# A transformer block on one core: all engines' instruction order taken from a simulated timeline

## The chip, the core and the metric

The kernel runs on one core of a Trainium2 chip. A core has five engines that each work through a queue of their own in order: TensorE (PE in the rows, with its weight loads as PEld), VectorE (DVE), ScalarE (ACT), GpSimd (POOL) and SyncE (SP), which here only starts DMA transfers. They wait for each other by semaphores. The metric is the device time of one execution in microseconds (us), as the median of several executions of the same program.

## What is computed

The reference is one block of a bidirectional encoder in float32, with 512 tokens, 16 learned meta tokens added (528 in all) and a model width of 1024. Cut to what matters:

```
h = concat([meta_tokens, x])
h = h + 0.5 * swiglu(rms_norm(h), w_gate, w_up, w_down)      # FFN 1, inner width 2816
z = rms_norm(h) @ w_in                                       # 10 parts, split by columns
y_a = hgrn2_bidir(...)      # gated linear recurrence, 4 heads of 128, both directions
y_b = axial_gqa(...)        # 8 query heads of 64 over 2 key heads, softmax over 528 keys
mixed = sigmoid(zgate_a) * (y_a @ w_up_a) + sigmoid(zgate_b) * (y_b @ w_up_b)
h = h + mixed @ w_out
h = h + 0.5 * swiglu(rms_norm(h), w_gate2, w_up2, w_down2)   # FFN 2
return h[meta:]
```

In `swiglu` the gate goes through silu and is multiplied with the up projection before the down projection. In `hgrn2_bidir` a head's gates come from sigmoids, and its recurrence is computed in chunks of 128 tokens.

## The kernel before

Everything is kept transposed: features on the 128 partitions, tokens along the free axis. A float32 product is made of three products of rounded parts: each weight tile `raw` (128 x 1024) is loaded by SP, rounded to `whi` by ACT (L84, the copy) and its remainder `wlo` is formed by DVE (L85, the subtraction). The activations are split in the same way (`xh`, `xl`). PE then multiplies `whi` with `xh`, `whi` with `xl` and `wlo` with `xh` into one PSUM bank (helper `group`, L197). `raw`, `whi` and `wlo` have two buffers each.

The program has three stages.

- **FFN 1** (function `ffn`): the first four columns of the inner width are plain groups. The other 18 are taken two at a time by `pair`, which forms the gate and up projections of two columns by a scheme with seven half-size products instead of eight (L374, products of 12 matmuls over 264 tokens each). The weights that it needs are partly sums of loaded tiles (`seven`, with sums on DVE at L110, L111, L117 and on POOL at L116). A down projection follows after each group of columns.
- **The mix**: the projections `w_in`, attention (`score`, `turned`, `product`) and the recurrence (`gla_head`, `gla_out`) are interleaved on PE by the class `Interleave`, with latencies given by hand (`LAT_...`). For this stage PE's order is the order in which the program is written; the other engines are left to the scheduler.
- **FFN 2**: as FFN 1, with 512 tokens.

What the names stand for that come up below: `R` is the reciprocal root of the mean square of a token (matmul with ones at L302, square root at L303, reciprocal at L304), by which each projection is multiplied when it leaves PSUM (L543). For a query, its squares (`tq`, L668) are summed by PE at L676, a Newton iteration on tiny tiles follows (`rsqrt`, L556 to L563: `xq`, `yq`, `aq`), and the rotary positions (`rope`, L600 to L603); `qst` holds the split query (L684, L685). A score is the bank pair `S` (L695); its maximum is `nm` (L699), its exponential `pr` (L704), its row sum `sm` (L706). The transposed `pr` goes from the bank `at` (L719) to `ph` and `pl` (L722, L723). In the recurrence a level copies `ks` (L882, ACT), multiplies it into the only bank `gs` (L886), multiplies `Z` on (L875 on DVE, L873 on POOL) and takes `gs` over into `A` by a predicated copy (L890). At the end of a head, `on` and `st` (L921, L927 to L929) feed the products of L940. The head's gates are the sigmoids of L810 and L811:

```
both = ap(Z, 0, ((3 * T, 2), (1, T)))
act.activation(both, both, AF.Sigmoid, scale=-1.0)
act.activation(Z[:, 1:3], zi, AF.Sigmoid)
```

Exponentials and sigmoids need different function tables on ACT; an ACT_TABLE_LOAD stands ahead of the first after a switch.

The order of the work is set in this way. The program is written once as one sequence. The tile framework gives every instruction its buffers and waits, and a scheduler then chooses each engine's order from the instructions whose operands it takes to be ready, those written first (or marked as of high priority, `OFFSET`) ahead. It goes by a simple estimate of when an operand is ready. In the mix PE is exempt: `tc.manual_schedule(engines={pe.engine})` (L528).

## Time and profile before

| what | value |
|---|---|
| median of 3 runs | 1199.37 us (1198.83 to 1202.58) |
| the profiled execution, whole | 1202.23 us |
| its span in the trace | 1200.4 us |
| PE busy | 1170.7 us, 98% of the span |
| DVE, ACT, POOL busy | 852.5, 583.3 and 188.2 us |
| loaded and stored | 106.22 MB, 88 GB/s on the mean |

The profiled execution is 1.83 us longer than its span (what lies before the first and behind the last instruction), and 0.24% above the median of the runs. PE is busy nearly all the time; whether another engine matters is to be read from the stretches in which PE is not.

### The profile page before, as it was taken

What the parts mean: (1) busy time and instruction counts of PE and PEld (TensorE: products, weight loads), DVE (VectorE), ACT (ScalarE), POOL (GpSimd) and SP (SyncE); (2) the same over time, 40 slices, a digit from 0 to 9 for tenths busy, and PEclk for the clock granted to TensorE, in tenths of its full rate; (3) what the DMA queues carried; (4) which work ended last, traced back from release to release, by engine and by line L of the source; (5) the groups of instructions that cost most, each with busy time, mean ns of one, the idle gap of its engine ahead of it and who ended that gap; (6) DMA issues with size and microseconds to landing.
All of it is one profiled execution on the core that took longest, in us unless ns stands there. A gap on an engine that the chain in (4) does not pass through costs nothing.

```text
span 1200.4 us, 19411 instructions
## 1 busy us (share of the span) xinstructions
PE 1170.7 (98%) x7765; PEld 1071.8 (89%) x7765; DVE 852.5 (71%) x1349; ACT 583.3 (49%) x984; POOL 188.2 (16%) x153
## 2 busy tenths in 40 slices
PE   8999999999999999999999999999999999999998
PEld 8999999999999788878888788888878998998997
DVE  7988748848956868787686735455788956866863
ACT  5545425524545475756557433334444633543541
POOL 1012001001102023243232410122001101101100
PEclk9999999999999999999999999999999999999999
DMA  6233222332223221111111113232413332333213
GB/s 233 63 100 136 89 89 96 108 95 90 80 67 120 70 71 36 53 36 54 36 54 36 61 46 112 81 118 94 156 55 121 104 102 97 107 100 108 90 54 123
DMA packets 34234, 106.22 MB, mean 88 GB/s; under 512 B 3936, under 2 KB 4320, under 8 KB 34144
## 3 DMA queue, kind: packets, MB, share of 16 engines
q1 hardware_dynamic: 33984, 104.44, 26.3%
q8 instruction: 61, 1.00, 0.3%
q0 software_dynamic: 160, 0.54, 0.1%
q14 instruction: 29, 0.24, 0.1%
HBM read 102.87 MB, written 2.10 MB: 87 GB/s over the span
## 4 chain that ended last, share of the span: by engine, by line
PE 81%; DVE 10%; ACT 5%; issue 2%; DMA 1%; POOL 0%; SPq 0%; ACTq 0%; DVEq 0%; POOLq 0%
PE mm L197 31%; PE mm L374 15%; PE at L374 9%; PE at L197 5%; PE gs L374 4%; PE am L197 4%; PE S L197 4%; PE am L374 2%; DVE wlo L85 2%; PE gs L886 2%; ACT whi L84 1%; PE mm L940 1%; PE mm L734 1%; PE S L695 1%; PE at L719 1%
## 5 line engine op out<-in xcount | busy, mean ns | idle before, releaser
L84 ACT CAST whi<-raw 128x1024 fp32r<-128x1024 f32 (+2 forms) x220 | 189.4, 862 | 286.4 <-PE mm L197 121.2
L85 DVE TENSOR_TENSOR wlo<-raw,whi 128x1024 fp32r<-128x1024 f32 (+2 forms) x220 | 225.1, 1025 | 27.8 <-ACT whi L84 22.3
L197 PE MATMUL mm<-xh,whi 128*128 128x512 f32 (+1 forms) x504 | 166.7, 364 | 5.5 <-ACT xh L278 2.2
L197 PE MATMUL mm<-xl,whi 128*128 128x512 f32 (+1 forms) x504 | 159.8, 351 | 0.5 <-DVE xl L279 0.5
L197 PE MATMUL mm<-xh,wlo 128*128 128x512 f32 (+1 forms) x504 | 159.1, 349 | 0.0
L116 POOL TENSOR_TENSOR sums<-raw 128x512 f32<-128x512 f32 x36 | 58.8, 1634 | 492.7 <-DVE wlo L85 492.7
L197 PEld LDWEIGHTS mm<-xh,whi 128*128 128x128 f32 x504 | 89.9, 191 | 18.5 <-ACT xh L278 2.4
L84 ACT CAST whi<-sums 128x1024 fp32r<-128x1024 f32 x72 | 75.4, 1051 | 62.3 <-DVE sums L111 20.9
L85 DVE TENSOR_TENSOR wlo<-sums,whi 128x1024 fp32r<-128x1024 f32 x72 | 87.6, 1219 | 24.9 <-ACT whi L84 24.7
L197 PEld LDWEIGHTS mm<-xh,wlo 128*128 128x128 f32 x504 | 89.0, 190 | 12.7 <-issue 0.2
L197 PEld LDWEIGHTS mm<-xl,whi 128*128 128x128 f32 x504 | 89.5, 191 | 10.6 <-DVE xl L279 1.0
L873 POOL TENSOR_TENSOR Z<-Z,tot 128x512 f32<-128x512 f32 x32 | 46.9, 1467 | 158.2 <-PE gs L886 94.4
L197 PE MATMUL mm<-hh,wlo 128*128 128x256 f32 (+1 forms) x218 | 63.0, 334 | 0.0
L197 PE MATMUL mm<-hh,whi 128*128 128x256 f32 (+1 forms) x218 | 62.8, 333 | 0.1
L197 PE MATMUL mm<-hl,whi 128*128 128x256 f32 (+1 forms) x218 | 62.9, 332 | 0.0
L374 PE MATMUL mm<-xl,whi 128*128 128x264 f32 (+1 forms) x216 | 61.3, 284 | 0.0
L374 PE MATMUL mm<-xh,whi 128*128 128x264 f32 (+1 forms) x216 | 61.2, 283 | 0.0
L374 PE MATMUL mm<-xh,wlo 128*128 128x264 f32 (+1 forms) x216 | 61.1, 283 | 0.0
L468 DVE SCALAR_TENSOR_TENSOR h<-mm,h 128x512 f32<-128x512 f32 (+2 forms) x40 | 21.0, 545 | 41.5 <-PE mm L197 41.5
L374 PE MATMUL at<-xh,whi 128*128 128x264 f32 (+1 forms) x144 | 42.0, 292 | 0.0
L197 PEld LDWEIGHTS mm<-hh,wlo 128*128 128x128 f32 x218 | 37.2, 188 | 4.5 <-DVE wlo L85 0.7
L197 PEld LDWEIGHTS mm<-hh,whi 128*128 128x128 f32 x218 | 37.4, 188 | 4.2 <-ACT whi L84 0.5
(365 smaller groups left out, 3377.7 us busy)
## 6 DMA issues: line engine op xcount, KB each, us to landing
raw<-in_wg SPq DMA_DIRECT2D x43, 512.0 KB, 3.7
raw<-in_wu SPq DMA_DIRECT2D x43, 512.0 KB, 3.2
raw<-in_w_in SPq DMA_DIRECT2D x42, 512.0 KB, 3.2
raw<-in_wd SPq DMA_DIRECT2D x48, 384.0 KB, 3.1
raw<-in_wd SPq DMA_DIRECT2D x16, 256.0 KB, 2.6
raw<-in_wup SPq DMA_DIRECT2D x16, 256.0 KB, 2.6
raw<-in_wout SPq DMA_DIRECT2D x8, 512.0 KB, 3.2
h<-in_xT SPq DMA_DIRECT2D x4, 528.0 KB, 6.6
```

The lines of the kernel that those rows point to most:

```text
L84: nc.scalar.copy(hi[:, c], src)
L85: nc.vector.tensor_tensor(lo[:, c], src, hi[:, c].bitcast(F32), ALU.subtract)
L116: nc.gpsimd.tensor_tensor(t[:, E], r0[:, E], r1[:, E], ALU.add)
L197: pe.matmul(o, a[:, sl], b[:, cols], start=(k == 0 and i == 0), stop=(k == n - 1 and i == 2))
L374: pe.matmul(o, a[:, sl], b[:, kk, :], start=(start and kk == 0 and i == 0), stop=(kk == 3 and i == 2), skip_group_check=True)
L468: dve.scalar_tensor_tensor(h[c][:, cols], o, 0.5, h[c][:, cols], ALU.mult, ALU.add)
L695: pe.matmul(s[:, WIDE][:, cols], st[e][:, c * P:(c + 1) * P], kk[:, cols], start=(i == 0), stop=(i == 1))
L719: pe.transpose(o[:, k, :], pr[:, k * P:(k + 1) * P], ident)
L734: pe.matmul(av, v[:, k, :], p[:, k, :], start=(k == 0 and i == 0), stop=False)
L873: pool.tensor_tensor(xx, xx, first, ALU.mult)
L886: pe.matmul(s[:, c, :], ks[:, c * P:(c + 1) * P], ap(Z, T + c * P, ((2 * m, P // (2 * m)), (T + m, 2), (1, m))), start=True, stop=True)
L940: pe.matmul(o[:, c, :], a, b, start=(i == 0), stop=(i == len(terms) - 1))
```

## The change

One argument is added where the tile context is made. The scheduler then runs a timeline of all engines as it goes, with an assumed duration for each instruction, and takes an operand to be ready when that timeline says so. It does so for all engines and all three stages. No instruction is added to or taken from the program, but for function tables on ACT: their number depends on the order.

```diff
-    with tile.TileContext(nc) as tc:
+    with tile.TileContext(nc, schedule_with_timeline_sim=True) as tc:
```

In the mix PE's order stays as it was written from the first query's sums (L676) to shortly before the stage's end. All other orders move: of the 1,300 to 1,350 rows of DVE most stand elsewhere by a few places.

**PE at the start of the first pair of FFN 1.** `mm_2162`, `mm_2163` and `mm_2164` are three banks of one pair, `whi_2075` and `wlo_2076` the parts of its first weight, `whi_2179` and `wlo_2180` those of its third, a sum; the rows begin where the last down projection ends. Before:

```order
L374 MATMUL mm_2162<-b11h_293,whi_2075 128x264
L374 MATMUL mm_2162<-b11l_294,whi_2075 128x264
L374 MATMUL mm_2162<-b11h_293,wlo_2076 128x264
L374 MATMUL mm_2162<-b11h_293,whi_2075 128x264
L374 MATMUL mm_2162<-b11l_294,whi_2075 128x264
```

And with the change:

```order
L374 MATMUL mm_2162<-b11h_293,whi_2075 128x264
L374 MATMUL mm_2162<-b11l_294,whi_2075 128x264
L374 MATMUL mm_2163<-b21h_295,whi_2075 128x264
L374 MATMUL mm_2163<-b21l_296,whi_2075 128x264
L374 MATMUL mm_2164<-n1h_297,whi_2179 128x264
L374 MATMUL mm_2164<-n1l_298,whi_2179 128x264
L374 MATMUL mm_2164<-n1h_297,wlo_2180 128x264
L374 MATMUL mm_2164<-n1h_297,whi_2179 128x264
L374 MATMUL mm_2164<-n1l_298,whi_2179 128x264
L374 MATMUL mm_2162<-b11h_293,wlo_2076 128x264
```

Seven matmuls that need no `wlo_2076` now stand ahead of the first that needs it, where `mm_2162` and `mm_2163` had been finished one after the other.

**ACT in the first head of the recurrence**, from the second score's scaled maximum on. Before:

```order
L701 ACTIVATE nr<-nm,yq 128x1
L810 ACT_TABLE_LOAD
L810 ACTIVATE Z<-Z 128x2x528
L704 ACT_TABLE_LOAD
L704 ACTIVATE pr,sm<-S,nr,yq 128x528
L722 CAST ph<-at 128x4x128
L707 ACTIVATE pr<-pr,sm 128x528
L811 ACT_TABLE_LOAD
L811 ACTIVATE Z<-zi 128x1056
L701 ACTIVATE nr<-nm,yq 128x1
L84 CAST whi<-raw 128x1024
L704 ACT_TABLE_LOAD
```

And with the change:

```order
L811 ACT_TABLE_LOAD
L811 ACTIVATE Z<-zi 128x1056
L810 ACTIVATE Z<-Z 128x2x528
L701 ACTIVATE nr<-nm,yq 128x1
L704 ACT_TABLE_LOAD
L704 ACTIVATE pr,sm<-S,nr,yq 128x528
L707 ACTIVATE pr<-pr,sm 128x528
L722 CAST ph<-at 128x4x128
L84 CAST whi<-raw 128x1024
L701 ACTIVATE nr<-nm,yq 128x1
```

The two sigmoids stand together, both ahead of the second exponential, and two of four table loads are gone (19 in the whole program before, 17 now).

**DVE in the second head of the recurrence**, between the products of the recurrence's levels (`gs_5891`, `gs_5931`), the rotary positions of a query (`tm_5659`, `tq_5878`) and two scores (`S_5900`, `S_5951`). Before:

```order
L602 SCALAR_TENSOR_TENSOR tq_5878<-tq_5878,par_92,cossin_4480 128x512
L561 TENSOR_TENSOR aq_5865<-yq_5864 128x8
L875 TENSOR_TENSOR Z_5088<-Z_5088,tot_5089 128x132x4
L562 SCALAR_TENSOR_TENSOR aq_5865<-aq_5865,xq_5863 128x8
L603 TENSOR_TENSOR tm_5659<-tm_5659,tq_5878 128x512
L563 SCALAR_TENSOR_TENSOR yq_5864<-aq_5865,yq_5864 128x8
L723 TENSOR_TENSOR pl_5832<-at_5940,ph_5831 128x4x128
L561 TENSOR_TENSOR aq_5865<-yq_5864 128x8
L699 TENSOR_REDUCE nm_5956<-S_5951 128x1
L562 SCALAR_TENSOR_TENSOR aq_5865<-aq_5865,xq_5863 128x8
L890 COPY_PREDICATED A_5732<-msk_64,gs_5931 128x512
```

And with the change:

```order
L890 COPY_PREDICATED A_5732<-msk_64,gs_5891 128x512
L601 SCALAR_TENSOR_TENSOR tm_5659<-tm_5659,par_92,cossin_4480 128x512
L602 SCALAR_TENSOR_TENSOR tq_5878<-tq_5878,par_92,cossin_4480 128x512
L699 TENSOR_REDUCE nm_5905<-S_5900 128x1
L559 TENSOR_SCALAR yq_5864<-yq_5864 128x8
L603 TENSOR_TENSOR tm_5659<-tm_5659,tq_5878 128x512
L561 TENSOR_TENSOR aq_5865<-yq_5864 128x8
L875 TENSOR_TENSOR Z_5088<-Z_5088,tot_5089 128x132x4
L890 COPY_PREDICATED A_5732<-msk_64,gs_5931 128x512
```

The predicated copy that empties the bank of `gs_5931` now follows directly on its `Z` product; the Newton steps and the next score's maximum that had stood between come behind it. The maximum of the score before, `nm_5905`, has gone the other way, behind L601 and L602.

## Rows read from the trace of the kernel before

**Rows 1.** The page: span, and busy time of each engine.

```profile
span 1200.4 us, 19411 instructions
...
PE 1170.7 (98%) x7765; PEld 1071.8 (89%) x7765; DVE 852.5 (71%) x1349; ACT 583.3 (49%) x984; POOL 188.2 (16%) x153
```

**Rows 2.** Busy time by stretch: us, PE, PEld, DVE, ACT, POOL, granted clock, DMA share, GB/s.

```profile
0.00:25.00 25.00, 21.12 (x135) 20.06 (x135) 17.57 (x25) 15.76 (x25) 4.63 (x7) 0.93 0.72 259
25.00:85.00 60.00, 59.67 (x481) 59.00 (x481) 54.78 (x115) 28.88 (x53) 0.93 (x1) 1.00 0.28 88
85.00:380.00 295.00, 293.64 (x2383) 291.65 (x2382) 212.91 (x306) 137.27 (x212) 36.06 (x24) 1.00 0.29 94
380.00:672.00 292.00, 271.44 (x1706) 237.57 (x1705) 216.23 (x405) 179.92 (x339) 79.25 (x77) 0.98 0.16 53
672.00:1160.00 488.00, 487.80 (x2876) 431.84 (x2875) 335.02 (x480) 213.05 (x345) 67.37 (x44) 1.00 0.29 96
```

**Rows 3.** PE's waits over the span: engine waited for, us in total, times, longest.

```profile
PE gs L886 <- ACT ks L882: 3.1, 3, 2.5
PE S L695 <- ACT pr L704: 2.7, 3, 1.6
PE S L695 <- DVE qst L685: 2.5, 1, 2.5
PE gs L886 <- ACT qst L684: 2.3, 1, 2.3
...
PE mm L940 <- DVE st L929: 2.1, 1, 2.1
...
PE at L374 <- DVE wlo L85: 1.4, 2, 0.7
```

**Rows 4.** Timeline at 184 us: start, us, engine, line, operation; idle before and releaser.

```profile
182.72 1.30 POOL L116 TENSOR_TENSOR sums<-raw 128x512 f32<-128x512 f32 x1 [4.16 <-DVE wlo L85]
182.84 2.26 DVE L85 TENSOR_TENSOR wlo<-raw,whi 128x1024 fp32r<-128x1024 f32 x1
...
185.16 0.39 PE L374 MATMUL at<-b11h,wlo 128*128 128x264 f32 x1 [0.65 <-DVE wlo L85]
...
186.31 1.21 DVE L85 TENSOR_TENSOR wlo<-sums,whi 128x1024 fp32r<-128x1024 f32 x1
```

**Rows 5.** Timeline at 436 us.

```profile
436.00 1.28 ACT L704 ACT_TABLE_LOAD   x1
...
437.30 0.79 ACT L704 ACTIVATE pr<-S,nr,yq 128x528 f32<-128x528 f32 x1
...
438.23 0.51 PE L695 MATMUL S<-kh,qst 128*128 128x256 f32 x2 [1.58 <-ACT pr L704]
```

**Rows 6.** Timeline at 465 us.

```profile
464.37 0.70 DVE L875 TENSOR_TENSOR Z<-Z,tot 128x528 f32<-128x528 f32 x1
...
465.60 0.60 ACT L882 COPY ks<-Z 128x512 f32<-128x512 f32 x1
...
466.26 1.01 PE L886 MATMUL gs<-Z,ks 128*128 128x128 f32 x3 [2.51 <-ACT ks L882]
```

**Rows 7.** Timeline at 532 us.

```profile
531.32 0.72 DVE L890 COPY_PREDICATED A<-msk,gs 128x512 f32<-128x512 uint8 x1
...
532.18 0.57 PE L886 MATMUL gs<-Z,ks 128*128 128x128 f32 x3 [2.29 <-ACT qst L684]
```

**Rows 8.** Timeline from 382 to 406 us.

```profile
382.13 3.45 DVE L304 RECIPROCAL R<-R 128x528 f32<-128x528 f32 x1
...
387.43 0.63 ACT L668 ACTIVATE tq<-tm 128x512 f32<-128x512 f32 x1 [2.77 <-DVE tm L543]
...
389.12 0.95 PE L676 MATMUL mm<-kones,tq 128*128 128x2 f32 x8
...
397.86 0.77 PE L197 MATMUL mm<-xh,whi 128*128 128x256 f32 x2 [1.22 <-ACT tm L623]
...
405.28 0.47 PE L197 MATMUL mm<-xh,whi 128*128 128x512 f32 x1 [1.05 <-DVE Z L543]
```

## The prediction

> **What bounds the kernel now.** I read the page first. PE is busy for 1170.7 of 1200.4 us [rows 1], so a new order can at best take away the 29.7 us in which it isn't. The table of stretches tells where they are: from 380 to 672 us, the mix with attention and recurrence, PE is busy for 271.44 of 292 us, so 20.6 us of the 29.7 lie there; from 85 to 380 us 1.4 us, from 672 to 1160 us 0.2 us, and 3.9 us in the first 25 us [rows 2]. DVE (216 of 292) and ACT (180 of 292) are far from full in the mix, so the idle time there is one of order and latency: an operation that PE needs stands behind others in DVE's or ACT's queue. That is what the change touches. In the FFNs it can only keep what is there or lose.
>
> The table of PE's waits gives the sizes: three waits of gs for ks, 3.1 us in all, of which one is 2.5; three of a score for the exponential before it, 2.7 us; one of a score for qst, 2.5; one at a gs put down to qst, 2.3; one for st, 2.1; and in FFN 1 two for wlo, 1.4 us [rows 3]. For each I looked at the timeline and then at what stands there in the changed order.
>
> **The change part by part.** No instruction is added, so every term is a wait that shrinks, grows or moves. The sum goes against the profiled execution of 1202.23 us.
>
> *Starts of pairs, FFN 1.* At 185.16 us PE waits 0.65 us for a wlo subtraction that took 2.26 us [rows 4]. An undisturbed one took 1.21; a POOL sum ran from 182.72 to 184.02, beside the first half of it [rows 4]. The Trainium skill ("SBUF — State Buffer", Who interferes with whom) has a DVE instruction with two inputs from SBUF blocked by a GpSimd one that reads SBUF, until that ends. The 2.26 us agree with it: 1.18 left of POOL's operation and 1.21 of its own would make 2.4. A scheduler whose assumed durations lack this places a wlo about 1 us early, and that rule is the strongest thing that speaks against the change (rival 3). In the changed order seven matmuls without that wlo stand ahead at the first pair, against two before. At the rate of the second stretch (481 in 59.67 us, 0.124 us each [rows 2]) five more cover 0.62 us. At the 0.65 us wait the changed order likewise puts five matmuls and a product's start ahead. Both waits go: -1.3 us (from 0 to -1.4).
>
> *Start and first columns.* DVE is busy for 54.8 of 60 us from 25 to 85 us, with 0.33 us of idle time on PE [rows 2]. The new order has DVE form all eight normalised tiles early, which pushes three wlo subtractions 2 to 4 us back, close to where PE needs them; matmuls of hi parts are pulled ahead as cover. I take +0.5 us. The bounds are 0 and three waits as long as the longest for wlo, 0.7 [rows 3], so +2.
>
> *Start of the mix.* The matmuls of the mean square (L302) go 18 places back on PE: eight of double width and ten at 0.124 us, about 3.2 us. Before, the reciprocal ran from 382.13 to 385.58, ACT squared the query from 387.43 to 388.06, and PE took it at 389.12 [rows 8]. A reciprocal that ends at 388.8, with its evacuation (about 0.65) and 0.63 for the square, gives 390.1: a new wait of 1.0 us. But the next wait of this chain, 1.22 us at 397.86 for a square root [rows 8], shrinks by as much, since that chain has not become later. Two evacuations that PE needs at 405.28 (1.05 us [rows 8]) and shortly after have moved ahead of wlo subtractions by about 4 us, and their waits go. I take -1.2 us (from +1.0, if only the delay shows, to -1.7).
>
> *Tables in the first head.* The wait of 1.58 us at 438.23 is for an exponential, ahead of which ACT loads a table for 1.28 us [rows 5]. With the sigmoids together that load is gone: -1.3 us. The exponential before it now has both sigmoids ahead, and by the durations of the rows ends about 0.5 us later: +0.5. Together -0.8 us (from +0.5 to -1.8). The Trainium skill ("ScalarE: Activation LUTs", What ACT_TABLE_LOAD costs) puts a switch at 1.28 us of load and 1.38 us of drain; the trace has the load, but the exponential starts 0.02 us behind it [rows 5], so no such drain shows as time after it. By the page the term would be -2.2 us.
>
> *First long wait for ks.* PE stands for 2.51 us until 466.26. The Z product ended at 465.07, but ACT took the copy only at 465.60, behind an exponential, and DVE had done a score's maximum first [rows 6]. In the changed order the copy stands ahead of the exponential and the product ahead of the maximum, about 0.7 to 1 us earlier. A copy from 464.4 to 465.0 instead of 465.60 to 466.20: -1.3 us (from 0 to -2.5, bounds of the row).
>
> *The bank of gs.* At 532.18 PE waits 2.29 us. The table names qst, but that is no operand of this matmul; the predicated copy that frees the only gs bank ended at 532.04 [rows 7]. It now stands before the tiny Newton steps and the next maximum, and by the rows' durations ends 2.3 us or more earlier: -2.0 us (at most -2.3). The maximum nm_5905 pays for it; its exponential then ends at about 526.7, 0.5 us before the next score needs the bank. If that is missed by its neighbour's stretch of about 1 us, the term keeps -1.5.
>
> *The wait for st* (2.1 [rows 3]): the addition comes about 0.8 us sooner, the copy ahead of it later, which moves part of the wait to the matmul before: -0.8 us (from 0 to -2.1). *The wait for qst* (2.5 [rows 3]): the rotary sum is earlier, but a subtraction and an evacuation still stand ahead on DVE: -0.7 us (from 0 to -2.5).
>
> The mix thus gives -1.2 - 0.8 - 1.3 - 2.0 - 0.8 - 0.7 = -6.8 us. Where PE comes sooner it meets the next wait sooner, and the three waits of scores for exponentials show that this chain has little slack [rows 3]; I take it that a third is given back, +2.3. With the FFN terms: -1.3 + 0.5 - 6.8 + 2.3 = -5.3 us. 1202.23 - 5.3 = 1196.9; the profiled execution is 0.24% above the median, so the median becomes 1194. All lower bounds together make some -14 us (1185), the upper ones +3 (1202).
>
> **The rivals.** A measurement of this kernel can tell about 0.3% (3.6 us) from no change.
>
> Rival 1, no change that can be measured: the waits only move. For it: PE's order in the mix is fixed, a score, its exponential and the next score share one bank, and a chain that needs its full time gives back what is gained before it. Against it: the largest waits end at an operation that stood ready behind others in a queue [rows 6, 7]. Two thirds given back, -2.3 - 0.8 = -3.1: about 1196.5; up to 1203.
>
> Rival 2, much more: DVE and ACT have 76 and 112 us to spare in the mix [rows 2], so a good order could remove nearly all of it. With 80% of the 20.6 us and the 1.3: 1202.2 - 17.8, as median 1181.6. Against it: the waits named above are only about 14 us of it, and several shrink only in part by the durations of the rows.
>
> Rival 3, slower: PE's new order at the starts of pairs meets wlo parts that are later than the scheduler takes them to be. There are 18 pairs (nine in each FFN), and only two wait now, 0.7 us each [rows 3]. The new order interleaves three products there, so a wlo that is late stops all of them, and it holds the two weight buffers longer. If each start waits 0.7 us, 18 x 0.7 = 12.6 in place of the 1.4: +11.2, with -4.5 from the mix +6.7, as median about 1206. It decides from some 0.5 us a start on, where it eats up the gain of 5.3 and 3.6 more. For it: a wlo beside a POOL sum takes 2.26 instead of 1.21 us [rows 4]. Against it: from 85 to 380 us and from 672 to 1160 PE has under 1.6 us of idle time [rows 2], so weights are mostly ready well before use.
>
> **How the numbers follow.** Chances: the forecast with its own range of 1189 to 1196, 0.48; rival 2 (below 1189), 0.08; rival 1 (1196 to 1203), 0.24; rival 3 and any other loss (above 1203), 0.20. The 0.3% bound is at 1195.8, so faster 0.55, same 0.25, slower 0.20. The range of 1187 to 1205 leaves out about 0.06 below and 0.14 above.
>
> **What would show it.** Busy time of PE from 380 to about 667 us unchanged at 271 us, with the stretch some 4 us shorter; no table load ahead of the exponential near 437 us and a score that waits under 0.5 us; the waits of gs together at about 2 us instead of 5.4; a wait of about 1 us before L676. The forecast is wrong if PE's idle time in the FFNs grows by more than 3 us, or if new waits in the mix (scores for exponentials above all) add up to what the old ones lose.

## The result and the profile after

The changed kernel is slower: 1207.0 us against 1201.58 us in the median of seven runs each, a ratio of 1.0051 (95% interval 1.0036 to 1.0065), about 5 to 6 us. Submitted once more it came out at 1.0035 (1.0022 to 1.0048). The forecast had been 1194 us. Single executions of one kernel lie up to 8 us apart (23 of the kernel before on one chip: 1197.15 to 1205.19), so a trace tells here where time goes, and the ratios tell how much: the two profiled executions, 1202.23 and 1204.65 us, differ by 2.4 us only, since the second is the fastest of its seven. Two single executions among the runs below took 2306 and 5030 us, far from all others, and no ratio counts them.

A lower clock does not explain the loss: in the second submission the mean granted clock is 0.995 over the six executions of the changed kernel and 0.995 over the 23 of the kernel before.

First the page of the changed kernel, in answer to [rows 1].

```profile
span 1202.8 us, 19362 instructions
...
PE 1170.9 (97%) x7765; PEld 1070.1 (89%) x7765; DVE 853.7 (71%) x1349; ACT 578.3 (48%) x982; POOL 188.0 (16%) x153
```

Then its table of stretches, in answer to [rows 2], with the long last stretch cut at 860 and 925 us.

```profile
0.00:25.00 25.00, 20.98 (x137) 19.78 (x138) 17.73 (x25) 15.53 (x25) 4.95 (x7) 0.93 0.65 241
25.00:85.00 60.00, 57.99 (x463) 56.85 (x462) 54.35 (x113) 27.28 (x52) 0.96 (x1) 1.00 0.30 95
85.00:380.00 295.00, 294.69 (x2402) 293.74 (x2402) 212.87 (x307) 138.17 (x214) 35.22 (x24) 1.00 0.29 95
380.00:672.00 292.00, 274.66 (x1732) 240.76 (x1732) 222.48 (x411) 182.11 (x343) 82.25 (x79) 0.99 0.15 52
672.00:860.00 188.00, 187.96 (x859) 154.68 (x858) 98.88 (x130) 68.29 (x107) 33.57 (x24) 1.00 0.28 100
860.00:925.00 65.00, 60.94 (x290) 50.31 (x289) 57.38 (x107) 30.29 (x58) 2.56 (x2) 0.97 0.26 84
```

From 380 to 672 us PE is busy for 274.7 us instead of 271.4: the mix lost idle time, but only 3.2 of its 20.6 us. From 25 to 85 us, the first columns of FFN 1, PE went from 59.67 to 57.99. And from 860 to 925 us, the plain columns of FFN 2, its first down projection and its first pair, PE stands for 4.1 us where from 672 to 1160 us it had been idle for 0.2 us in all. Total busy time is unchanged.

PE's queue holds the same instructions in both programs, so the start of the n-th matmul, changed minus before, shows how far PE is behind by then. Worked out from the traces at six places (each entry is what PE loses, or gains with a minus, from the place before; in us; the order differs a little around them, which moves a value by up to 0.3):

| trace | columns of FFN 1 (to n = 600) | pairs of FFN 1 (to 2900) | attention and recurrence (to 4700) | rest of the mix (to 5500) | columns and first pair of FFN 2 (to 5950) | rest (to the end) |
|---|---|---|---|---|---|---|
| changed | +2.0 | -3.0 | -4.7 | +0.2 | +5.6 | +2.3 |
| changed, second trace | +4.1 | -2.8 | -4.7 | +0.3 | +5.5 | +2.3 |

By this table the mix and the pairs of FFN 1 give what was forecast or more (a part of the -4.7 is not the order's doing, see below). It is taken back where the plain columns stand in the two FFNs, and in the rest of FFN 2.

PE's waits in the mix, in answer to [rows 3]:

```profile
PE mm L914 <- DVE yb L739: 3.2, 1, 3.2
PE S L695 <- ACT pr L704: 2.5, 3, 2.0
...
PE mm L676 <- issue: 1.5, 1, 1.5
PE mm L197 <- DVE vs L660: 1.4, 1, 1.4
...
PE gs L886 <- ACT ks L882: 1.0, 2, 0.5
...
PE S L695 <- DVE qst L685: 0.6, 1, 0.6
PE gs L886 <- DVE yq L563: 0.4, 1, 0.4
```

The waits of gs at L886 went from 5.4 to 1.4 us by this table, that for qst from 2.5 to 0.6. The wait for yb grew from 0.2 to 3.2 us, and 1.5 at L676 (put down to nothing that the profile shows) and 1.4 for L660 are new.

And PE's waits from 860 to 925 us, where the kernel before has none:

```profile
PE at L374 <- ACT whi L84: 1.9, 1, 1.9
PE mm L197 <- DVE wlo L85: 1.2, 2, 0.8
PE mm L197 <- ACT whi L84: 0.5, 1, 0.5
PE am L197 <- DVE hl L273: 0.4, 1, 0.4
```

All but one (`hl`, the second part of a column's result) are for parts of weights. DVE's timeline ahead of the first two shows where it was in the meantime:

```profile
858.30 0.69 DVE L449 TENSOR_TENSOR g<-mm,R 128x512 f32<-128x512 f32 x1
858.90 0.68 DVE L452 TENSOR_TENSOR u<-mm,R 128x512 f32<-128x512 f32 x1
859.50 5.38 DVE L331 SCALAR_TENSOR_TENSOR xn<-h,par,R 128x512 f32<-128x512 f32 x8
864.80 0.68 DVE L449 TENSOR_TENSOR g<-at,R 128x512 f32<-128x512 f32 x1
...
866.33 1.22 DVE L85 TENSOR_TENSOR wlo<-raw,whi 128x1024 fp32r<-128x1024 f32 x1
```

The next two rows, from ACT and PE, are of the same moments:

```profile
860.91 1.04 ACT L84 CAST whi<-raw 128x1024 fp32r<-128x1024 f32 x1
...
867.60 0.50 PE L197 MATMUL mm<-xh,wlo 128*128 128x512 f32 x1 [0.35 <-DVE wlo L85]
```

The eight normalisations L331 all become ready when R does. The new order runs them as one block of 5.4 us. The whi for the next wlo was there at 861.95; the subtraction started at 866.33, 4.4 us later, and ended when PE had been at this group of matmuls since 865.40. In the kernel before L331 stands in ones and twos from 858.71 to 878.91, and the same weight is treated so:

```profile
858.71 1.41 DVE L331 SCALAR_TENSOR_TENSOR xn<-h,par,R 128x512 f32<-128x512 f32 x2
...
865.59 1.06 ACT L84 CAST whi<-raw 128x1024 fp32r<-128x1024 f32 x1 [1.22 <-PE at L197]
...
866.68 1.23 DVE L85 TENSOR_TENSOR wlo<-raw,whi 128x1024 fp32r<-128x1024 f32 x1
...
871.01 0.39 PE L197 MATMUL mm<-xh,whi 128*128 128x512 f32 x1
```

There the wlo began 1.1 us after its whi began and was ready at 867.91, 3.1 us before PE came to it. In FFN 1 the new order runs L331 as two, five and one, and the first wlo behind them starts at 36.27 us, where it started at 32.33 before.

### The profile page after: what moved, and what is told of

Same layout as the page of the kernel before. It is cut to its first block, busy times and chain, and to the rows that moved or that the text cites. A ratio compares the mean times of both kernels' runs of the same rounds, so it can differ in the third digit from the quotient of the medians.

```text
span 1202.8 us, 19362 instructions
## 1 busy us (share of the span) xinstructions
PE 1170.9 (97%) x7765; PEld 1070.1 (89%) x7765; DVE 853.7 (71%) x1349; ACT 578.3 (48%) x982; POOL 188.0 (16%) x153
## 4 chain that ended last, share of the span: by engine, by line
PE 48%; DVE 5%; ACT 2%; issue 1%; DMA 0%; ACTq 0%; DVEq 0%
PE mm L197 23%; PE mm L374 8%; PE at L374 4%; PE at L197 3%; PE gs L374 2%; PE am L197 2%; PE gs L886 1%; PE am L374 1%; PE mm L940 1%; PE mm L734 1%; DVE wlo L85 1%; ACT whi L84 1%; PE S L695 1%; PE at L719 1%; DMA raw<-in_wu 0%
## 5 line engine op out<-in xcount | busy, mean ns | idle before, releaser
L85 DVE TENSOR_TENSOR wlo<-raw,whi 128x1024 fp32r<-128x1024 f32 (+2 forms) x220 | 217.5, 998 | 20.4 <-ACT whi L84 19.7
L197 PE MATMUL mm<-xh,whi 128*128 128x512 f32 (+2 forms) x504 | 168.1, 364 | 6.9 <-ACT xh L278 2.0
L197 PE MATMUL mm<-xh,wlo 128*128 128x512 f32 (+2 forms) x504 | 161.7, 352 | 0.4 <-DVE wlo L85 0.4
L197 PE MATMUL mm<-xl,whi 128*128 128x512 f32 (+2 forms) x504 | 160.7, 350 | 0.0
L197 PEld LDWEIGHTS mm<-xh,whi 128*128 128x128 f32 x504 | 90.6, 192 | 20.4 <-issue 3.1
L85 DVE TENSOR_TENSOR wlo<-sums,whi 128x1024 fp32r<-128x1024 f32 x72 | 87.3, 1220 | 17.2 <-ACT whi L84 17.1
L273 DVE TENSOR_TENSOR hl<-u,hh 128x528 fp32r<-128x528 f32 (+1 forms) x44 | 36.8, 837 | 11.8 <-ACT hh L272 11.8
```

What stands on the lines that cost most here:

```text
L85: nc.vector.tensor_tensor(lo[:, c], src, hi[:, c].bitcast(F32), ALU.subtract)
L197: pe.matmul(o, a[:, sl], b[:, cols], start=(k == 0 and i == 0), stop=(k == n - 1 and i == 2))
L273: dve.tensor_tensor(dst[1][:, cols], src[:, cols], dst[0][:, cols].bitcast(F32), ALU.subtract)
```

## The experiments

In each run the time is compared with that of the kernel before on the same chip.

**The changed kernel once more** (no edit).

> The changed kernel once more, for a second trace and an interval. Theory A (the loss lies in the FFNs, where weight parts come later than the new order of PE takes them to be, while the mix gains some 4.5 us): ratio 1.003 to 1.006, and the waits for whi and wlo at the first columns of both FFNs (about 69 us, 866 to 915 us) are there again. Rival (the trace caught one late load, of 5.2 us at 909 us): the wait of 1.9 us at the first pair of FFN 2 is gone, and the ratio is 1.000 to 1.003.

Measured: 1.0035 (1.0022 to 1.0048). The same waits stand at the same instructions: from 860 to 925 us 2.1 us for wlo, 1.9 for whi at the first pair, 0.7 and 0.4. Where the loss is, is no accident of one trace.

**PE in written order in the FFNs**, with the timeline and without:

```diff
+            with tc.manual_schedule(engines={pe.engine}):
-            ffn(ft, xt, C_FFN1, T, last1)
+                ffn(ft, xt, C_FFN1, T, last1)
```

and the same around FFN 2; the control has the flag of the change off.

> The changed kernel, with PE in the order in which the program is written in the two FFNs as well; the other engines go by the timeline. Theory A, PE's interleaved order does it: the losses in the FFNs go, the mix keeps its gain, so 4 to 5 us faster than before, ratio 0.996. Rival B, the order on DVE and ACT does it (evacuations ahead of weight parts): the losses stay, ratio 1.004 or more, since PE then has no filler either.

> The kernel before, with PE in written order in the FFNs: the control to the run with the timeline. If PE's own order matters little where the others go by the estimate: ratio 0.999 to 1.002. If the fillers that the scheduler finds for PE are worth something: 1.003 to 1.008, with waits for wlo at the starts of pairs.

Measured: 1.0143 (1.0129 to 1.0158) with the timeline, 1.0025 (1.0014 to 1.0035) without. Theory A falls: PE's interleaving isn't the harm. With PE held to the written order the timeline's orders on the other engines cost 17 us by the trace: 10.5 in the columns of FFN 1 and 9.6 in the columns and first pair of FFN 2, less what the mix gives; without the timeline the same PE order costs 2.1 and 0.5 there. So the harm is in the queues of the other engines, and PE's new order is a cover that hides a good part of it.

**A third raw buffer:**

```diff
-        raw = self.pool.tile([P, 1024], F32, name="raw", tag="raw", bufs=2)
+        raw = self.pool.tile([P, 1024], F32, name="raw", tag="raw", bufs=3)
```

with TX from 640 to 608 to make room, and the two loads of `seven` alike.

> The changed kernel with three buffers for raw instead of two (xh and xl padded 2 KB less to make room). Theory C, loads start late because a raw buffer is freed only by a later wlo: loads go out earlier, the waits at the first columns of both FFNs shrink, and the time falls by 4 us or more against the changed kernel, ratio to before 0.996 to 1.001. Theories A and B (order, not loads): as the changed kernel, 1.004 to 1.006.

> The kernel before with three buffers for raw (same padding change): the control to the run with the timeline, which came out about 0.2% faster than the changed kernel. If late loads are a matter of the new order: ratio 0.999 to 1.001 here. If a third buffer helps any order: 0.997 to 0.999.

Measured: 1.0021 (1.0010 to 1.0031) with the timeline, 0.9998 (0.9986 to 1.0010) without. Against the changed kernel on the same chip (1.0035) the buffer recovers 1.7 us, with intervals that overlap; under the old order it recovers nothing. In its trace the wait of 1.9 us at the first pair is gone, and the waits at the columns of FFN 2 stand (0.5 and 0.7 us). A raw buffer is freed when its wlo is done, so a late wlo delays the load after next too: late loads look like a follow-up of late wlo, not the root, and a run below bears on that.

**Written order on more engines:** as above, with `{pe, dve, act, pool}` and with `{dve}` alone.

> The changed kernel with PE, DVE, ACT and POOL in written order in the two FFNs (from their first columns on); the start and the mix go by the timeline. Theory B (the timeline's order on DVE and ACT puts evacuations and splits ahead of weight parts; PE's new order only softens it): the FFNs come within 3 us of before and the mix keeps its 4.7 us, so ratio 0.997 to 1.000. Rival A (PE needs the timeline's fillers whatever DVE does): as with PE alone in written order, 1.010 or more.

> The changed kernel with DVE alone in written order in the FFNs; PE and ACT follow the timeline. Theory B, with DVE as the engine that does it: the 5.6 us at the first columns and first pair of FFN 2 shrink below 2 us, ratio 0.996 to 1.000. If it is ACT's order (the copies to whi) or PE's: no better than the changed kernel, 1.003 or more.

Measured: 1.1252 (1.1232 to 1.1272) and 1.0989 (1.0971 to 1.1008). Both misses: the written order on DVE is far worse than either scheduler's. In the second, PE's longest groups of waits are for whi and wlo, 19.8 us in 18 and 16.1 us in two. They show how much hangs on where wlo stands in DVE's queue, but don't tell the two theories apart.

**The sigmoids in the other order**, in the kernel before:

```diff
-                    act.activation(both, both, AF.Sigmoid, scale=-1.0)
                     act.activation(Z[:, 1:3], zi, AF.Sigmoid)
+                    act.activation(both, both, AF.Sigmoid, scale=-1.0)
```

> The kernel before with the sigmoid of L811 written ahead of that of L810, nothing else. If the table load ahead of the exponential is the cause of the wait of 1.58 us at 438 us: one or two table loads fewer and that wait under 0.5 us, ratio 0.998 to 1.000. If the wait only moves (a later exponential, a later Z): ratio 1.000, with as much at the score before, near 431 us.

Measured: 0.9992 (0.9980 to 1.0005). Inconclusive: the scheduler kept an exponential between the two, 19 table loads stayed, and so did the wait, 1.64 us at 438.65. The price of the table load was not isolated.

**The normalisations held back.** That left the block of L331. A tiny DVE operation copies the gains of a column and also reads (times zero) the result of the column before; L331 takes its gain from the copy, and so becomes ready column by column, as in the order before.

```diff
-            def early(kk):
+            def early(kk, dep=None):
+                gk = par
...
+                if dep is not None:
+                    gk = ft.tile([P, 64], F32, name="gk", tag="gk", bufs=2)
+                    dve.scalar_tensor_tensor(gk[:, gain:gain + KT], dep[:, :KT], 0.0, par[:, gain:gain + KT], ALU.mult, ALU.add)
                 for k in (kk, kk + 4):
-                    dve.scalar_tensor_tensor(xn[:, k], h[k][:, :n], par[:, gain + k:gain + k + 1], R[:, :n],
+                    dve.scalar_tensor_tensor(xn[:, k], h[k][:, :n], gk[:, gain + k:gain + k + 1], R[:, :n],
...
-                    early(j)
+                    early(j, dep)
+                    dep = u
```

> The changed kernel, with each column's pair of L331 in the two FFNs held back until the column before it is done (a tiny copy of the gains that also reads that column's result). Theory D: all eight L331 become ready with R at one moment, the timeline puts them in one block of 5.3 us on DVE, and the wlo behind them come 4 us late; that is where the FFNs lose. Then the waits for whi and wlo at the first columns of both FFNs go, PE is 4 to 6 us earlier by the first pair of FFN 2 than in the changed kernel, and the ratio to before is 0.996 to 1.000. Rival E, the loss is from the order at the down projections and pair starts (PE's matmuls pulled ahead): no more than 1.5 us better than the changed kernel, 1.002 to 1.005.

> The kernel before with the same hold: the control. DVE's order there already has two L331 at a time, so both theories expect 0.999 to 1.001; the tiny copies add six DVE operations of some 0.1 us, off PE's path.

Measured: 0.9996 (0.9983 to 1.0008) with the timeline, 1.0000 (0.9986 to 1.0014) without. The loss is gone with the hold, and the hold alone does nothing. The trace of the first is not used here; the run further below (`held_again`) has another. The opposite, all eight written in one block in the kernel before:

```diff
-                for k in (kk, kk + 4):
+                for k in range(KT) if not kk else ():
                     dve.scalar_tensor_tensor(xn[:, k], h[k][:, :n], par[:, gain + k:gain + k + 1], R[:, :n],
```

> The kernel before with all eight L331 written in one block behind R in each FFN: the one part of the change alone, without the timeline. Theory D: PE waits for wlo at the first columns of both FFNs as in the changed kernel, 1 to 4 us in the first and 2 to 4 us in the second, ratio 1.002 to 1.006. Rival E: 0.999 to 1.001.

Measured: 1.0039 (1.0024 to 1.0055). The block alone makes the kernel before as slow as the change does. In FFN 1 DVE ran the eight as three, two and three with one operation between, and the wlo that had started at 32.33 us started at 38.96. PE's waits for wlo in its first 110 us:

```profile
PE at L197 <- DVE wlo L85: 4.7, 2, 4.3
```

One wait of 4.3 us in FFN 1; in FFN 2 none, against expectation: there the scheduler split the eight into three, one, two and two, with a wlo behind the fourth, so that no block arose and this run says nothing of FFN 2. Hence the question which FFN bears the loss under the timeline, and the last three runs.

> The changed kernel with the hold and with three raw buffers. If late loads and the block of L331 add up: 2 us below the hold alone, ratio 0.995 to 0.998. If the third buffer helped only against the block: equal to the hold alone.

Measured: 1.0003 (0.9991 to 1.0016). With the hold the third buffer gives nothing more (0.9996 without it): what it helped, it helped against the block.

> The changed kernel with the hold on L331 in both FFNs once more, since the trace of the first such run was disturbed. Theory D: no wait of PE over 0.9 us from 860 to 925 us, where the changed kernel has 3.9 to 5.1 us in all, and none over 0.5 us at 36 to 39 us; ratio 0.998 to 1.001 as in the first run. If the wait of 1.9 us for whi at the first pair of FFN 2 is still there: it has another cause (PE's matmuls pulled ahead).

> The changed kernel with the hold on L331 in FFN 1 alone. The block without the timeline cost 5 us in FFN 1 and nothing in FFN 2; if that is how the two share the loss under the timeline too: ratio 0.998 to 1.001. If the trace's shares hold (2 to 4 us in FFN 1, 5.6 us in FFN 2): only a part of the gain, 1.001 to 1.003.

> The changed kernel with the hold on L331 in FFN 2 alone. By the shares of the trace: 4 us better than the changed kernel, ratio 1.000 to 1.002, with the waits of FFN 1 unchanged. If FFN 1 holds it all: as the changed kernel, 1.003 to 1.005.

Measured: 0.9995 (0.9982 to 1.0008) with the hold in both, 1.0019 (1.0009 to 1.0029) in FFN 1 alone, 1.0017 (1.0005 to 1.0030) in FFN 2 alone. Each FFN bears some 0.2%, and the two add up: from 1.0035 to 1.0051 without a hold, by about 0.002 with one of them, to 0.9995; each of these steps is uncertain by about 0.0015. At 36 to 39 us PE waits no longer (0.6 and 0.3 us in the changed kernel), as expected. PE's waits from 860 to 925 us with the hold in both, all there are:

```profile
PE mm L197 <- DVE wlo L85: 0.8, 1, 0.8
PE am L197 <- DVE hl L273: 0.3, 1, 0.3
```

1.1 us, where the changed kernel has 4.0 by the rows above and 5.1 in its second trace; the wait of 1.9 us at the first pair is gone with the block (with the hold in FFN 1 alone it stands, 1.6 us). In the table's terms PE loses 0.6 us in the columns and first pair of FFN 2 instead of 5.6. But a new wait for wlo comes just behind that window, at the next pair:

```profile
931.35 0.38 PE L377 MATMUL mm<-b11h,wlo 128*128 128x256 f32 x1 [1.20 <-DVE wlo L85]
```

So over the whole of FFN 2 the loss goes from 7.9 us to 4.3 in the traces, 3.6 us less, where the times have 2.9. In FFN 1 the traces don't show the gain: the hold takes the two waits at 37 us away, but waits of 0.2 to 1.4 us stand at starts of pairs then, where the changed kernel has one of 0.3 or 0.6. There the times alone speak for it.

## Why the prediction was wrong

**The step that failed** is the costing of the FFNs, above all of FFN 2, for which the sum has no term. I had read from PE's 0.2 us of idle time there that there was nothing to gain, and that "weights are mostly ready well before use". They were (3.1 us in the rows above), but by the old order of DVE: the same function runs in FFN 2, the block stands there too, and it took that lead away. By the ratios it costs 0.0024 (1.0019 to 0.9995), 2.9 us, with intervals that leave 1 to 5; in the traces PE loses 5.6 us up to the first pair and 2.3 behind it.

The other part is *Start and first columns*. It named the right mechanism for FFN 1 ("the new order has DVE form all eight normalised tiles early, which pushes three wlo subtractions 2 to 4 us back") and priced it at +0.5 us, on the trust that matmuls pulled ahead would cover it. They cover most: without them it is 10.5 us. But holding L331 back in FFN 1 is worth 0.0022 (1.0017 to 0.9995), 2.6 us with intervals that leave 0.5 to 5, and the traces have +2.0 and +4.1 in these columns: more than my +0.5, and whether it is beyond my upper bound of +2 is not shown. These two make 5.5 us, about the whole loss: with both held, the change is neither faster nor slower. That spreading out L331 is what kept PE busy is shown for FFN 1 by the block in the kernel before, for FFN 2 by the hold alone.

The sign of being wrong that the prediction names came: PE's idle time in the FFNs grew by 1.7 us from 25 to 85 us and by 3.9 from 860 to 925, and shrank by 1.1 from 85 to 380.

**Rival 3** was the nearest: PE meets weight parts later than the scheduler takes them to be. Its place was wrong (18 starts of pairs; PE waits at one in FFN 2, and in FFN 1 two waits went away and one of 0.3 us came) and so was its cause (POOL beside DVE; it was DVE's own queue). The timeline orders by the moment of readiness, and here eight operations that were ready at once went as one block, or nearly one, ahead of a wlo that PE was about to need.

**Starts of pairs, FFN 1:** forecast -1.3. Both waits are gone, and PE gains 2.8 to 3.0 us over the pairs: right, and what made it larger is not shown. The order that is printed as that of the first pair stands in the trace at the fourth, at 182.7 us, which is the one with the wait of 0.65 us; nine matmuls are ahead of its first wlo there, not seven. At the first pair, at 85.7 us, two are ahead as before.

**Tables in the first head:** forecast -0.8. The wait of 1.58 us is gone, that at the score before rose from 0.79 to 1.96 us: -0.4. All 19 table loads in the trace of the kernel before take 1.28 us, and ACT's next operation starts 0.01 us behind each: the drain that the prediction weighed shows at none of them.

**Wait for ks:** forecast -1.3; from 2.51 to 0.50 us, -2.0. **The bank of gs:** forecast -2.0; from 2.29 to 0.51, -1.8. **The wait for st:** forecast -0.8; gone, with 1.4 us at the matmul before it, -0.7. **The wait for qst:** forecast -0.7; from 2.50 to 0.55, -1.9. These four were read rightly from the rows in place and sign; the first and the last gave more than forecast.

**Start of the mix:** forecast -1.2, and wrong. The wait at L676 came (1.5 us for 1.0), but the one of 1.22 for the square root stayed, since its chain is later too; the waits at 405 and 410 us went, and 0.9 and 1.4 came at 412 and 413 us. Summed +2.0.

**Given back:** a third, +2.3, was taken as a lump, without naming the waits. The terms above sum to -4.8 and all waits of the mix to -3.1, so +1.7 was given back; that this is near the lump is luck, since one wait alone grew by more, to 3.2 us for yb. Timeline of the changed kernel:

```profile
488.83 1.81 POOL L819 TENSOR_TENSOR zg<-zi,Z 128x512 f32<-128x512 f32 x1 [4.80 <-ACT Z L811]
...
489.40 1.80 DVE L875 TENSOR_TENSOR Z<-Z,tot 128x512 f32<-128x512 f32 x1
...
490.23 0.58 ACT L738 COPY ta<-mm 64x512 f32<-64x512 f32 x1
...
491.12 1.67 DVE L815 TENSOR_SCALAR tot<-Z,noml 128x512 f32<-128x512 f32 x2
...
494.03 0.69 DVE L739 TENSOR_TENSOR yb<-mm,ta 64x512 f32<-64x512 f32 x1
...
494.78 0.28 PE L914 MATMUL mm<-ident,Z 128*16 128x128 f32 x1 [3.24 <-DVE yb L739]
```

L739 had its operand at 490.81 and stood behind four groups on DVE until 494.03. The L875 among them took 1.80 us beside a POOL operation; [rows 6] has one at 0.70. That is the rule of the Trainium skill ("SBUF — State Buffer", Who interferes with whom) that the prediction weighed, and the trace agrees; no run here shows what the order would be with these durations in it.

Over the mix, PE's waits of over 0.15 us sum to 20.4 us before and 17.2 after: -3.1, where the forecast had -4.5. The -4.7 of the table is more than the waits explain, because the trace of before also has a lower granted clock there (0.98 over the stretch, 0.99 in the changed kernel). Stretch from 385 to 680 us, before:

```profile
385.00:680.00 295.00, 274.44 (x1720) 240.11 (x1719) 220.50 (x410) 180.51 (x339) 81.43 (x74) 0.98 0.15 51
```

and in the control with held normalisations:

```profile
385.00:680.00 295.00, 274.53 (x1748) 240.25 (x1748) 224.50 (x414) 183.26 (x343) 82.33 (x75) 1.00 0.16 52
```

The waits are the same there (20.4 and 20.2 us), and busy time too, but the control's trace is through with attention and recurrence 4.8 us sooner, with a clock of 1.00 for 0.98.

**What stays open:** with the hold in both FFNs PE's waits in the mix sum to 14.9 us in the trace, 5.5 less than before, and the pairs of FFN 1 give 1.5. That should leave the change some 5 us faster or more; measured is 0.5 us. The trace places 3.7 us of the difference in the rest of FFN 2 (1.2 of it the new wait at 931 us) and 2.5 in the start and columns of FFN 1, with waits for weights of 0.2 to 1.2 us each at pair starts and down projections. In the changed kernel itself PE loses 2.3 us in the rest of FFN 2, of which waits of over 0.15 us explain 0.6. No experiment took these apart.

## What to carry to other kernels

An order made by readiness can put everything that becomes ready at one moment into one block, and what a busy engine hands to PE then comes late by up to the block's length. So look for the places where many operations wait for one value, and ask what stands behind them in the queue. A stage without idle time has nothing to gain from a new order and all of its cover to lose: it belongs into the sum, with the lead that each weight has before it is used. If such an order is wanted for another stage, a tiny false dependency that lets the many become ready one by one can take the harm away; here it brought the time back to that of the kernel before, and no lower.

## What the runs showed of the hardware

A wait can cost more than its length. Behind the wait of 1.9 us at 915 us the granted clock fell; the stretches before and behind it in the changed kernel:

```profile
900.00:915.00 15.00, 13.28 (x61) 10.89 (x59) 10.61 (x19) 6.24 (x10) 1.27 (x1) 1.00 0.34 107
915.00:925.00 10.00, 9.84 (x69) 9.84 (x70) 8.53 (x11) 4.04 (x7) 1.29 (x1) 0.83 0.30 105
```

0.83 over 10 us is a loss of 1.7 us of PE's work on top of the wait: for a part of the stretch the clock was at the lower of its two levels (1.2 instead of 2.4 GHz), and the matmuls behind the wait follow each other at 0.21 us instead of 0.12. Behind the wait of 4.3 us in the kernel before with the block it was more; there 7 us at 0.51 lose 3.4:

```profile
39.00:46.00 7.00, 5.77 (x26) 5.77 (x27) 7.00 (x16) 2.24 (x5) 0.00 (x0) 0.51 0.46 151
```

It does not follow every wait. In the second trace of the changed kernel the same wait of 1.9 us ends at 918.64 us, and the clock stays full:

```profile
915.00:925.00 10.00, 8.13 (x61) 7.54 (x60) 8.40 (x10) 4.34 (x6) 2.57 (x2) 1.00 0.16 56
```

The two traces from 385 to 680 us with equal waits differ in the same way. How much this makes in a time is seen in the kernel before: of its 32 executions beside the runs of the hold, the seven with a mean granted clock of 0.998 have a median of 1199.3 us, the five with 0.994 one of 1202.8.

And one load of 512 KB, of wu at 909 us in the changed kernel, took 5.2 us to land in both of its traces, where the median of this line's 43 loads on its page is 3.4 us. It is the load for which the first pair of FFN 2 waits. With the hold in FFN 1 alone it took 5.0 us, in FFN 2 alone 3.2; with the hold in both it took 4.7, and PE did not wait. Why is open.
